# The first mixer of a two-block kernel: biases, products on ones, shift columns, and GpSimd's share of the splits

## The chip, the cores and the metric

The kernel runs on one core of one Trainium2 chip. The metric is the device time of one execution in microseconds. A core has five engines that run beside each other: TensorE (PE in the profile; PEld are its weight loads), VectorE (DVE), ScalarE (ACT), GpSimd (POOL) and SyncE (SP), which here only issues transfers (DMAs).

## The reference

Two transformer blocks over one sequence of 256 tokens of 1024 features. The change is in the first mixer, the first half of the first block:

```
mod = silu(c) @ w_ada + b_ada                  # 6 parts of 1024: sh1, sc1, g1, sh2, sc2, g2
h = rmsnorm(x, gain0) * (1 + sc1) + sh1
proj = h @ w_in                                # qa, ka, va (512 each), qb (512), kb, vb (128 each)
out_a = attention of 8 heads of 64 (causal, position bias)
out_b = windowed attention of 8 heads over 2 key heads, with sinks
x = x + g1 * rmsnorm(concat(out_a, out_b) @ w_out, gain1)
```

The second half is a feed-forward layer with its own scale and shift (sc2, sh2). The second block has two mixers and a mixture of 16 experts, whose weights (16 times 24 MB) are most of what is read.

## The kernel before

**Weights.** All weights pass through `Weights`: `unit` lists the transfers in the order of use, `pump` issues the next one on SyncE's queue as soon as its arena of SBUF chunks (1 MB each) has room, `done` gives chunks back when the last reader is through. Matrix products are made of three products of a rounded upper part and a remainder: `convert` casts a slice to its upper part on ScalarE (L228) and takes the remainder on VectorE or, for the slice numbers in `POOL_SPLITS`, on GpSimd (L232). Two slices are prepared ahead (`LOOK`). `mm3` issues upper x upper, upper x remainder and remainder x upper (L311 to L313).

**The modulation.** Six parts of `mod` are computed from `w_ada`. "sc" and "sh" come in four quarters of 1 MB, `quarter_step` makes their products on TensorE (L486) after two products that bring in the bias (L480); `summed` copies the sums out, `quarter_cols` turns them into columns of `modT` (L499, L501). "as" does the same in halves (`pe_step`, bias at L529, products at L534). "s2", "gA" and "ag" are accumulated on VectorE (L518), from a tile that GpSimd clears and fills with the bias (`begin`).

**The order of the first mixer.** x is normalised and transposed (xT); the scale's sums give A1 (L722). The keys (L746) run on xT scaled by A1, without the shift, in four groups k2 with three passes each; the quarters of the shift are put between the groups, and the product that makes the table of position biases (L760, L764, L776) after the third group. With the shift known, `scaled` writes the whole h = xT * A1 + sh as upper part and remainder (L664 to L666); the shift's product with the key weights is made apart (`shift_row`, L807, `shift_cols`, L817) and added to the keys as a bias. The queries `qa` (four tiles of 24 products) then run on h. After them `drive` interleaves two generators: `attention` (scores L903, softmax L914 to L934, transposes L944, values L958) and `proj_rest` (va, kvb, qb, the remaining parts of the modulation, the first half of w_out), as many steps of the second after each step of the first as `ATTENTION` says. The scaling of the softmax by the reciprocal sums is on GpSimd (L934). A tile of small vectors, VC, is transposed and copied on VectorE (L848) before the attention.

The tile framework puts each engine's instructions in an order of its own by estimated times and dependencies; `behind` names instructions after which the following ones are to be issued. Each engine works its queue in order.

Of the kernel before, what the change touches and what calls it, by code (L numbers as in the profile page):

```python
# [29 lines left out]
POOL_SPLITS = ((8, 10, 13, 15, 16, 17),  # L30
# [12 lines left out]
class Weights:  # L43
# [167 lines left out]
    def convert(self, upto):  # L211
        while self.conv < min(upto, len(self.slices)):
# [19 lines left out]
            eng.tensor_tensor(lo, src, hi.bitcast(F32), op=ALU.subtract)  # L232
# [28 lines left out]
def block_kernel(ctx: ExitStack, tc: tile.TileContext, x, c, w_in, w_out, sinks, rel_bias, w_ada, b_ada,  # L261
# [167 lines left out]
    bada = mod.tile([12, 512], F32, name="bada")  # L429
    nc.sync.dma_start(bada, b_ada[0].rearrange("(r f) -> r f", f=512))  # L430
# [4 lines left out]
    hsh = sp.tile([128, 8, S], F32R, name="hsh")  # L435
# [17 lines left out]

    p = tp_ps((128, 8))
# [13 lines left out]
    modT = const.tile([128, 48], F32, name="modT")  # L468
# [4 lines left out]
    def quarter_step(name, i, ps):  # L473


        t = W.raw(f"{name}{i}")
        if i == 0:
            r = 2 * PARTS.index(name)
            for j in range(2):
                mm(ps[32 * j:32 * j + 32, :], ident[0:12, r + j:r + j + 1].to_broadcast([12, 32]), bada,  # L480
                   start=True, stop=False, tile_position=(0, 32 * j))
        for kk in range(2):
            k = 2 * i + kk
            for j in range(2):
                b = 64 * kk + 32 * j
                mm(ps[b:b + 32, :], sc[:, k, :], t[:, kk, j * 512:(j + 1) * 512],  # L486
                   start=(k == 1), stop=(k >= 6))
        W.done(f"{name}{i}")
# [7 lines left out]
    def quarter_cols(name, m):  # L496
        ps = tp_ps((128, 4, 2))
        for b in range(4):
            mm(ps[:, b, :], m[:, b * 128:(b + 1) * 128], pairs, start=True, stop=True)  # L499
        i = 8 * PARTS.index(name)  # L500
        nc.vector.tensor_copy(modT[:, i:i + 8].rearrange("p (j b) -> p b j", j=2), ps)  # L501

    def begin(name, acc):

        if name in PE_PARTS:
            return
        ACC[name] = acc() if callable(acc) else acc
        acc = ACC[name]
        nc.gpsimd.memset(acc, 0.0)
        nc.gpsimd.dma_start(acc[0:1, :], flat(b_ada, D * PARTS.index(name), [[0, 1], [1, D]]))  # L510

    def step(name, i):
# [4 lines left out]
        for kk in range(w):  # L517
            nc.vector.scalar_tensor_tensor(ACC[name], t[:, kk, :], sc[:, w * i + kk, 0:1], ACC[name],  # L518
                                           op0=ALU.mult, op1=ALU.add)
        W.done(f"{name}{i}")  # L520

    def pe_step(name, i):
# [3 lines left out]
        if i == 0:  # L526
            r = 2 * PARTS.index(name)
            for j in range(2):
                mm(ps[32 * j:32 * j + 32, :], ident[0:12, r + j:r + j + 1].to_broadcast([12, 32]), bada,  # L529
                   start=True, stop=False, tile_position=(0, 32 * j))  # L530
        for kk in range(4):
            for j in range(2):
                b = 64 * (kk % 2) + 32 * j
                mm(ps[b:b + 32, :], sc[:, 4 * i + kk, :], t[:, kk, j * 512:(j + 1) * 512],  # L534
                   start=(kk == 1 if i == 0 else kk < 2), stop=(kk >= 2))
# [9 lines left out]
    def cols(name):  # L545
        if name in PE_PARTS:
            ps = tp_ps((128, 4, 2))
            for b in range(4):
                mm(ps[:, b, :], M[name][:, b * 128:(b + 1) * 128], pairs, start=True, stop=True)
            i = 8 * PARTS.index(name)  # L550
            nc.vector.tensor_copy(modT[:, i:i + 8].rearrange("p (j b) -> p b j", j=2), ps)
            return
# [4 lines left out]
        nc.vector.tensor_copy(modT[:, i:i + 8], ps)  # L557
# [136 lines left out]
    nc.vector.tensor_copy(nT, p0)  # L694
    for t in range(2):
# [24 lines left out]
    quarter_cols("sc", summed(msc))  # L720
    A1 = const.tile([128, 8], F32, name="A1")
# [8 lines left out]
    hs = (hsh, ap_.tile([128, 8, S], F32R, name="hsl", tag="ol"))  # L730
    kp = [b_ps((128, 256)) for _ in range(4)]

    def key_operands(k2):
        w = W.take(f"ka{k2 // 2}", 0)
        for k in (2 * k2, 2 * k2 + 1):
            nc.scalar.activation(hs[0][:, k, :], xT[:, k, :], AF.Copy, scale=A1[:, k:k + 1])
            nc.vector.scalar_tensor_tensor(hs[1][:, k, :], xT[:, k, :], A1[:, k:k + 1],
                                           hs[0][:, k, :].bitcast(F32), op0=ALU.mult, op1=ALU.subtract)
        return w

    def keys(k2, w, passes):
        for a, b in passes:
            for kk in range(2):
                k = 2 * k2 + kk
                for m in range(4):
                    mm(kp[m], w[a][:, kk, m * 128:(m + 1) * 128], hs[b][:, k, :],  # L746
                       start=(k == 0 and (a, b) == (0, 0)), stop=(k == 7 and (a, b) == (0, 1)))
# [9 lines left out]
    keys(2, ops[2], ALL)  # L757

    p = tp_ps((16, 384))
    mm(p, rb, pos, start=True, stop=True)  # L760
    bdist = sp.tile([16, 384], F32, name="bdist", tag="junk1")
    nc.vector.tensor_copy(bdist, p)
    fd = dram.tile([16, 384], F32, name="fd")
    nc.gpsimd.dma_start(fd, bdist)  # L764
# [4 lines left out]
    h = scaled(xT, A1, modT[:, 0:8])  # L769
# [50 lines left out]
    row = shift_row(["ka0", "ka1"], modT[:, 0:8], mod, "acc", 2)  # L820
    s0.close()
    wox = at.enter_context(tc.tile_pool(name="wox", bufs=2))
    as_ = ExitStack()
    aw = as_.enter_context(tc.tile_pool(name="attnw", bufs=2))
# [10 lines left out]
    qa = fm_block("qa", 4, h, put_q(0))  # L835
    next(qa)
# [7 lines left out]
    run(qa)  # L844
# [60 lines left out]
    def attn_soft(i):  # L905
# [144 lines left out]
    A2 = const.tile([128, 8], F32, name="A2")  # L1050
# [751 lines left out]
```

## Time and profile before

| | |
|---|---|
| median of 3 runs | 1499.63 us (1499.04 to 1503.82) |
| the profiled execution | 1499.25 us, its span 1497.5 us |
| TensorE, busy | 1120.5 us (75%) |
| VectorE, ScalarE, GpSimd, busy | 471.0, 303.9, 242.9 us |
| bytes moved | 513.59 MB, 343 GB/s over the span |
| mean clock granted to TensorE | 0.876 of full speed |

The span runs from the first to the last instruction; the rest of the execution's time lies around it. Busy shares are means over stages with different limits, so they are read stage by stage. The clock column of a stretch is the mean over two levels, 1.0 (2.4 GHz) and 0.5 (1.2 GHz).

### The profile page before, as it was taken

What the parts mean: (1) busy time and instruction counts of PE and PEld (TensorE: products, weight loads), DVE (VectorE), ACT (ScalarE), POOL (GpSimd) and SP (SyncE); (2) the same over time, 40 slices, a digit from 0 to 9 for tenths busy, and PEclk for the clock granted to TensorE, in tenths of its full rate; (3) what the DMA queues carried; (4) which work ended last, traced back from release to release, by engine and by line L of the source; (5) the groups of instructions that cost most, each with busy time, mean ns of one, the idle gap of its engine ahead of it and who ended that gap; (6) DMA issues with size and microseconds to landing.
All of it is one profiled execution on the core that took longest, in us unless ns stands there. A gap on an engine that the chain in (4) does not pass through costs nothing.

```text
span 1497.5 us, 16937 instructions
## 1 busy us (share of the span) xinstructions
PE 1120.5 (75%) x7125; PEld 625.3 (42%) x7125; DVE 471.0 (31%) x910; ACT 303.9 (20%) x535; POOL 242.9 (16%) x233
## 2 busy tenths in 40 slices
PE   7889999999989999964665665655656655665566
PEld 4675788897988896211111111111111111111122
DVE  3586667666788755100000000000000000000003
ACT  4436453454464652000000000000000000000000
POOL 1251253433335462000000000000000000000001
PEclk9999999999999999987788778888778879778887
DMA  9878346464335578999999999999999999999996
GB/s 359 306 296 297 112 172 239 173 222 170 121 137 202 196 281 328 415 431 433 430 429 430 432 426 433 430 431 426 432 427 433 432 428 431 431 428 432 433 418 233
DMA packets 69510, 513.59 MB, mean 343 GB/s; under 512 B 6178, under 2 KB 11443, under 8 KB 52026
## 3 DMA queue, kind: packets, MB, share of 16 engines
q1 hardware_dynamic: 67706, 508.27, 82.5%
q0 software_dynamic: 1440, 3.71, 0.8%
q8 instruction: 56, 0.92, 0.3%
q10 hardware_dynamic: 288, 0.52, 0.1%
q14 instruction: 20, 0.16, 0.0%
HBM read 511.42 MB, written 1.07 MB: 342 GB/s over the span
## 4 chain that ended last, share of the span: by engine, by line
DMA 49%; PE 37%; DVE 7%; POOL 2%; ACT 2%; issue 1%; POOLq 0%; SPq 0%; ACTq 0%; DVEq 0%
DMA wd<-in_w_down_e_dram 16%; DMA wd<-in_w_gate_e_dram 16%; DMA wd<-in_w_up_e_dram 16%; PE tp L1649 6%; PE f L1667 3%; PE f L311 3%; PE f L313 3%; PE f L312 3%; PE big L313 3%; PE big L312 3%; PE big L311 3%; DVE cy L1240 1%; DMA wa<-in_w_up_e_dram 1%; PE big L746 1%; PE tp L311 1%
## 5 line engine op out<-in xcount | busy, mean ns | idle before, releaser
L1649 PE MATMUL tp<-wa,work 128*32 128x512 f32 x1000 | 148.6, 744 | 105.3 <-DMA wa<-in_w_up_e_dram 82.2
L1657 DVE TENSOR_TENSOR work<-work,tp 128x512 f32<-128x512 f32 x16 | 11.0, 688 | 562.4 <-PE tp L1649 562.4
L1660 POOL TENSOR_SCALAR work<-iot,gi 128x256 f32<-128x256 f32 x16 | 14.8, 924 | 822.7 <-PE big L1701 805.2
L228 ACT CAST wboth<-wa 128x1024 fp32r<-128x1024 f32 x116 | 120.4, 1045 | 112.3 <-PE f L313 48.8
L1649 PE MATMUL tp<-wd,work 128*32 128x512 f32 x568 | 93.9, 797 | 62.6 <-DMA wd<-in_w_gate_e_dram 33.9
L232 DVE TENSOR_TENSOR wboth<-wa,wboth 128x1024 fp32r<-128x1024 f32 x92 | 116.3, 1271 | 56.3 <-ACT wboth L228 56.1
L311 PE MATMUL f<-hTh,wboth 128*128 128x256 f32 (+1 forms) x448 | 131.3, 293 | 2.6 <-ACT wboth L228 1.6
L313 PE MATMUL f<-hTh,wboth 128*128 128x256 f32 (+1 forms) x448 | 130.0, 290 | 2.2 <-DVE wboth L232 2.2
L312 PE MATMUL f<-hTl,wboth 128*128 128x256 f32 (+1 forms) x448 | 129.3, 289 | 0.0
L1649 PEld LDWEIGHTS tp<-wa,work 128*32 128x32 f32 x1000 | 35.3, 132 | 215.7 <-DMA wa<-in_w_up_e_dram 96.5
L1667 PE MATMUL f<-wa,work 128*32 128x512 f32 x472 | 74.3, 778 | 60.5 <-DMA wa<-in_w_down_e_dram 60.4
L1697 ACT ACTIVATE work<-f,gi 128x512 f32<-128x512 f32 x15 | 10.3, 687 | 537.0 <-PE f L1667 537.0
L1649 PE MATMUL tp<-we,work 128*32 128x512 f32 x384 | 62.8, 794 | 37.9 <-DMA we<-in_w_gate_e_dram 24.8
L311 PEld LDWEIGHTS f<-hTh,wboth 128*128 128x128 f32 x448 | 88.0, 196 | 4.1 <-ACT wboth L228 2.0
L1698 DVE TENSOR_SCALAR work<-f,gi 128x512 f32<-128x512 f32 x15 | 11.3, 750 | 248.0 <-PE f L1667 248.0
L313 PEld LDWEIGHTS f<-hTh,wboth 128*128 128x128 f32 x448 | 88.0, 196 | 2.7 <-DVE wboth L232 2.7
L312 PEld LDWEIGHTS f<-hTl,wboth 128*128 128x128 f32 x448 | 88.1, 197 | 0.1
L1649 PEld LDWEIGHTS tp<-wd,work 128*32 128x32 f32 x568 | 21.9, 141 | 132.2 <-issue 54.6
L232 POOL TENSOR_TENSOR wboth<-wa,wboth 128x1024 fp32r<-128x1024 f32 x24 | 59.3, 2475 | 65.6 <-ACT wboth L228 65.6
L1667 PE MATMUL f<-wd,work 128*32 128x512 f32 x256 | 49.6, 869 | 26.8 <-DMA wd<-in_w_down_e_dram 26.8
L1656 ACT ACTIVATE work<-tp 128x512 f32<-128x512 f32 x16 | 9.6, 597 | 292.4 <-PE tp L1649 292.4
L1667 PEld LDWEIGHTS f<-wa,work 128*32 128x32 f32 x472 | 19.6, 138 | 108.2 <-issue 103.8
(518 smaller groups left out, 1953.5 us busy)
## 6 DMA issues: line engine op xcount, KB each, us to landing
wa<-in_w_up_e_dram SPq DMA_DIRECT2D x15, 4096.0 KB, 33.8
wa<-in_w_down_e_dram SPq DMA_DIRECT2D x14, 4096.0 KB, 33.6
wa<-in_w_gate_e_dram SPq DMA_DIRECT2D x14, 4096.0 KB, 34.2
wa<-in_w_in_dram SPq DMA_DIRECT2D x14, 2048.0 KB, 7.5
wd<-in_w_down_e_dram SPq DMA_DIRECT2D x7, 4096.0 KB, 33.7
wd<-in_w_up_e_dram SPq DMA_DIRECT2D x7, 4096.0 KB, 33.6
wa<-in_w_dram SPq DMA_DIRECT2D x12, 2048.0 KB, 7.5
we<-in_w_gate_e_dram SPq DMA_DIRECT2D x8, 3072.0 KB, 36.0
```

The lines of the kernel that those rows point to most:

```text
L228: self.last = self.nc.scalar.copy(hi, src)
L232: eng.tensor_tensor(lo, src, hi.bitcast(F32), op=ALU.subtract)
L311: mm(o, a[0], b[0], start=start, stop=False)
L312: mm(o, a[0], b[1], start=False, stop=False)
L313: mm(o, a[1], b[0], start=False, stop=stop)
L746: mm(kp[m], w[a][:, kk, m * 128:(m + 1) * 128], hs[b][:, k, :], start=(k == 0 and (a, b) == (0, 0)), stop=(k == 7 and (a, b) == (0, 1)))
L1240: nc.vector.scalar_tensor_tensor(ys[k], zc[:, k, j:j + 256], vc(VC_CW, 8 * j + k), ys[k], op0=ALU.mult, op1=ALU.add)
L1649: LAST["pe"] = mm(ps[32 * j:32 * j + 32, :], xe[:, k, :], t[:, j * 512:(j + 1) * 512], start=(k == 0), stop=(k == 7))
L1657: nc.vector.tensor_tensor(hid, hid, pu, op=ALU.mult)
L1660: nc.gpsimd.tensor_scalar(oht, iot, gi[:, 1, e:e + 1], None, op0=ALU.is_equal)
L1667: mm(ps[32 * r:32 * r + 32, :], hT[:, 4 * j + r, :], ts[r][:, a:a + n], start=(j == 0), stop=(j == 3))
L1698: nc.vector.tensor_scalar(ye[1], pd[1], gi[:, 0, e:e + 1], None, op0=ALU.mult)
```

## The change

All edits are in the first mixer.

- *Biases.* `b_ada` is loaded as 48 rows of 128, transposed once on TensorE (`badaT`), and added where the columns are copied to `modT`. The bias products in `quarter_step` and `pe_step` and, for "s2", GpSimd's clearing and bias load go; the first step of "s2" writes the accumulator instead of adding to it.
- *Products on ones.* `warm_up` multiplies a tile of ones by a tile of ones into a bank that nobody reads: twelve products of 128 columns at the start, one of 256 columns behind the scale's sums, two behind the scale's columns.
- *The table product* is issued behind the keys of the third group.
- *Queries.* They run on the keys' operands `hs` (xT * A1), which get two more columns that hold the shift; a product of 258 columns gives the queries without the shift and, in column 256, the shift's part, which is scaled on VectorE and added as a bias on the way out (ScalarE). `scaled` still makes h for the later projections, behind the splits made so far. `shift_row` comes after the first tile of queries, and the pool of the keys' operands is closed after the queries.
- *GpSimd.* The six slices of the first mixer that it split go to VectorE; so does the softmax's scaling, as four instructions with a scalar per partition in place of two with a broadcast.
- `modT`, `A1` and `A2` move to another pool.

```diff
-POOL_SPLITS = ((8, 10, 13, 15, 16, 17),
+POOL_SPLITS = ((),
...
-            eng.tensor_tensor(lo, src, hi.bitcast(F32), op=ALU.subtract)
+            self.last_lo = eng.tensor_tensor(lo, src, hi.bitcast(F32), op=ALU.subtract)
...
-    bada = mod.tile([12, 512], F32, name="bada")
-    nc.sync.dma_start(bada, b_ada[0].rearrange("(r f) -> r f", f=512))
+    bada = sp.tile([48, 128], F32, name="bada")
+    nc.sync.dma_start(bada, b_ada[0].rearrange("(r f) -> r f", f=128))
...
+    def warm_up(n, w):
+
+        ps = b_ps()
+        for _ in range(n):
+            mm(ps[:, 0:w], ones, ones_w[:, 0:w], start=True, stop=True)
+
+    ones_w = sp.tile([128, 256], F32, name="ones_w")
+    nc.vector.memset(ones_w, 1.0)
+    warm_up(12, 128)
...
-        if i == 0:
-            r = 2 * PARTS.index(name)
-            for j in range(2):
-                mm(ps[32 * j:32 * j + 32, :], ident[0:12, r + j:r + j + 1].to_broadcast([12, 32]), bada,
-                   start=True, stop=False, tile_position=(0, 32 * j))
...
-        nc.vector.tensor_copy(modT[:, i:i + 8].rearrange("p (j b) -> p b j", j=2), ps)
+        nc.vector.tensor_tensor(modT[:, i:i + 8].rearrange("p (j b) -> p b j", j=2), ps,
+                                badaT[:, i:i + 8].rearrange("p (j b) -> p b j", j=2), op=ALU.add)
...
+    p0 = tp_ps((128, 48))
+    nc.tensor.transpose(p0, bada, ident[0:48, 0:48])
+    badaT = gpp.tile([128, 48], F32, name="badaT")
+    nc.vector.tensor_copy(badaT, p0)
...
-    quarter_cols("sc", summed(msc))
+    msc = summed(msc)
+    with behind("sums"):
+        warm_up(1, 256)
+    quarter_cols("sc", msc)
+    with behind("cols"):
+        warm_up(2, 256)
...
-    p = tp_ps((16, 384))
-    mm(p, rb, pos, start=True, stop=True)
...
+    with behind("keys"):
+
+        p = tp_ps((16, 384))
+        mm(p, rb, pos, start=True, stop=True)
...
-    h = scaled(xT, A1, modT[:, 0:8])
+    shift = modT[:, 0:8].rearrange("p (k o) -> p k o", o=1).to_broadcast([128, 8, 2])
+    nc.vector.tensor_copy(hs[0][:, :, S:HW], shift)
+    nc.vector.tensor_tensor(hs[1][:, :, S:HW], shift, hs[0][:, :, S:HW].bitcast(F32), op=ALU.subtract)
     keys(3, ops[3], ALL[1:])
...
-    qa = fm_block("qa", 4, h, put_q(0))
-    next(qa)
+
+    def queries(m):
+
+        ps = (f_ps, tp_ps)[m % 2]((128, HW))
+        fm_tile("qa", hs, ps)
+        bq = wk.tile([128, 1], F32, name="bq", tag="ms", bufs=4)
+        nc.vector.tensor_scalar(bq, ps[:, S:S + 1], 0.125, None, op0=ALU.mult)
+        nc.scalar.activation(qT[:, m, :].rearrange("p (t n) -> p t n", t=2),
+                             rev(ps[:, 0:S].rearrange("p (t n) -> p t n", t=2)), AF.Identity, scale=0.125, bias=bq)
+
+    queries(0)
+    row = shift_row(["ka0", "ka1"], modT[:, 0:8], mod, "acc", 2)
+    LAST["hi"], LAST["lo"] = W.last, W.last_lo
+    with behind("hi", "lo"):
+        h = scaled(xT, A1, modT[:, 0:8])
+    queries(1)
...
-    run(qa)
+    for m in range(2, 4):
+        queries(m)
+    s0.close()
...
-        for b, (o, n) in enumerate(((0, 128), (128, 256))):
-            nc.gpsimd.tensor_tensor(L[:, :, o:o + n], L[:, :, o:o + n],
-                                    rs[:, :, b:b + 1].to_broadcast([128, 2, n]), op=ALU.mult)
+        for u in range(2):
+            for b, (o, n) in enumerate(((0, 128), (128, 256))):
+                nc.vector.tensor_scalar(L[:, u, o:o + n], L[:, u, o:o + n], rs[:, u, b:b + 1], None, op0=ALU.mult)
```

## Rows read from the trace of the kernel before

**Rows 1.** The page: chain that ended last, shares by engine.
```profile
DMA 49%; PE 37%; DVE 7%; POOL 2%; ACT 2%; issue 1%; POOLq 0%; SPq 0%; ACTq 0%; DVEq 0%
```

**Rows 2.** Busy time by stage; last columns: clock, share of transfers, GB/s.
```profile
24.90:43.80 18.90, 18.83 (x128) 14.87 (x128) 7.27 (x12) 5.73 (x10) 1.57 (x2) 0.85 1.03 390
...
66.76:158.65 91.89, 84.81 (x517) 61.08 (x516) 69.40 (x140) 44.86 (x113) 31.54 (x23) 0.94 0.71 267
...
598.00:1497.00 899.00, 560.36 (x3534) 152.97 (x3534) 69.88 (x136) 22.48 (x35) 19.30 (x20) 0.81 0.99 421
```

**Rows 3.** The same view in two microseconds each, for the clock.
```profile
24.00:26.00 2.00, 1.07 (x5) 1.07 (x6) 1.97 (x5) 1.63 (x3) 0.52 (x1) 0.50 1.03 410
84.00:86.00 2.00, 2.00 (x7) 1.71 (x6) 1.66 (x4) 1.35 (x4) 0.08 (x1) 0.50 0.95 336
```

**Rows 4.** Timeline before the keys: start, length, engine, line, [idle before it, ended by].
```profile
21.86 1.04 ACT L228 CAST wboth<-wa 128x1024 fp32r<-128x1024 f32 x1 [4.20 <-DMA wa<-in_w_in_dram]
...
22.51 0.81 PE L760 MATMUL tp<-pos,rb 34*16 34x384 f32 x2
...
24.93 0.58 PE L746 MATMUL big<-hsh,wboth 128*128 128x256 f32 x1 [1.07 <-ACT hsh L736]
```

**Rows 5.** Timeline from the shift's sums to the first whole query product.
```profile
43.83 0.42 DVE L492 COPY m<-f 128x256 f32<-128x256 f32 x1 [10.27 <-PE f L486]
...
45.39 0.17 DVE L501 COPY modT<-tp 128x8 f32<-128x8 f32 x1 [0.81 <-PE tp L499]
...
45.62 1.92 PE L807 MATMUL f<-wa,modT 128*32 128x512 f32 x16 [0.26 <-DVE modT L501]
...
50.16 1.05 PE L817 MATMUL tp<-quad,row 128*128 128x1 f32 x8 [2.62 <-ACT row L811]
...
53.35 0.58 PE L313 MATMUL f<-hTh,wboth 128*128 128x256 f32 x1 [1.47 <-DVE wboth L232]
```

**Rows 6.** Timeline around TensorE's longest wait of the attention stage.
```profile
79.65 2.65 DVE L919 TENSOR_SCALAR nm<-mx 128x4 f32<-128x4 f32 x1
79.91 2.35 POOL L232 TENSOR_TENSOR wboth<-wa,wboth 128x1024 fp32r<-128x1024 f32 x1
82.21 1.27 DVE L518 SCALAR_TENSOR_TENSOR acc<-wa,sc,acc 128x1024 f32<-128x1024 f32 x1
...
83.71 0.90 PE L944 MATMUL tp<-ident,L 128*128 128x128 f32 x3 [3.92 <-DVE VC L848]
```

**Rows 7.** Timeline of VectorE: scaling 512 columns in SBUF.
```profile
9.06 0.49 DVE L700 TENSOR_SCALAR xn<-X,rs 128x512 f32<-128x512 f32 x1 [0.24 <-POOL rs L589]
```

**Rows 8.** Transfers of the first 70 us: count, size, median us to landing.
```profile
wb<-in_w_ada_dram SPq DMA_DIRECT2D x2, 1024.0 KB, 16.1
```

**Rows 9.** Timeline of issues: third and fourth shift quarter, bias tables.
```profile
17.00 2.86 SPq L149 DMA_DIRECT2D wb<-in_w_ada_dram  x2
...
29.16 1.57 POOL L776 DMA_DIRECT2D tb<-fd  x2 [4.45 <-DMA fd<-bdist]
```

**Rows 10.** Groups by shape, 60 to 165 us: count | busy, mean ns | idle.
```profile
L518 DVE SCALAR_TENSOR_TENSOR acc<-wa,sc,acc 128x1024 f32<-128x1024 f32 x12 | 17.8, 1483 | 0.2
...
L232 POOL TENSOR_TENSOR wboth<-wa,wboth 128x1024 fp32r<-128x1024 f32 x6 | 15.5, 2588 | 16.2 <-ACT wboth L228 16.1
L232 DVE TENSOR_TENSOR wboth<-wa,wboth 128x1024 fp32r<-128x1024 f32 x12 | 14.8, 1254 | 8.6 <-ACT wboth L228 8.6
...
L934 POOL TENSOR_TENSOR L<-L,rsm 128x512 f32<-128x512 f32 x8 | 10.3, 1283 | 0.0
...
L919 DVE TENSOR_SCALAR nm<-mx 128x4 f32<-128x4 f32 x8 | 4.5, 561 | 0.2
...
L529 PE MATMUL f<-bada,ident 12*32 12x512 f32 x4 | 2.4, 672 | 0.0
```

**Rows 11.** Timeline of TensorE among the queries, first and last of 56.
```profile
60.13 0.28 PE L313 MATMUL f<-hTh,wboth 128*128 128x256 f32 x1
...
66.56 0.28 PE L313 MATMUL f<-hTh,wboth 128*128 128x256 f32 x1
```

More of the change, by code (lines that the diff above doesn't have):

```diff
@@ L485, in quarter_step @@
                 b = 64 * kk + 32 * j
-                mm(ps[b:b + 32, :], sc[:, k, :], t[:, kk, j * 512:(j + 1) * 512],
-                   start=(k == 1), stop=(k >= 6))
+                LAST["sums"] = mm(ps[b:b + 32, :], sc[:, k, :], t[:, kk, j * 512:(j + 1) * 512],
+                                  start=(k < 2), stop=(k >= 6))
         W.done(f"{name}{i}")
@@ L498, in quarter_cols @@
         for b in range(4):
-            mm(ps[:, b, :], m[:, b * 128:(b + 1) * 128], pairs, start=True, stop=True)
+            LAST["cols"] = mm(ps[:, b, :], m[:, b * 128:(b + 1) * 128], pairs, start=True, stop=True)
         i = 8 * PARTS.index(name)
-        nc.vector.tensor_copy(modT[:, i:i + 8].rearrange("p (j b) -> p b j", j=2), ps)
+        nc.vector.tensor_tensor(modT[:, i:i + 8].rearrange("p (j b) -> p b j", j=2), ps,
+                                badaT[:, i:i + 8].rearrange("p (j b) -> p b j", j=2), op=ALU.add)
     def begin(name, acc):
@@ L507, in begin @@
         ACC[name] = acc() if callable(acc) else acc
+        if name == "s2":
+            return
         acc = ACC[name]
@@ L517, in step @@
         for kk in range(w):
+            if name == "s2" and i == kk == 0:
+                nc.vector.tensor_scalar(ACC[name], t[:, 0, :], sc[:, 0, 0:1], None, op0=ALU.mult)
+                continue
             nc.vector.scalar_tensor_tensor(ACC[name], t[:, kk, :], sc[:, w * i + kk, 0:1], ACC[name],
@@ L525, in pe_step @@
         ps = f_ps()
[L526 to L530, printed above, removed]
         for kk in range(4):
@@ L534, in pe_step @@
                 mm(ps[b:b + 32, :], sc[:, 4 * i + kk, :], t[:, kk, j * 512:(j + 1) * 512],
-                   start=(kk == 1 if i == 0 else kk < 2), stop=(kk >= 2))
+                   start=(kk < 2), stop=(kk >= 2))
         W.done(f"{name}{i}")
@@ L546, in cols @@
         if name in PE_PARTS:
[L547 to L552, printed above, removed]
+            return quarter_cols(name, M[name])
         ps = tp_ps((128, 8))
@@ L735, in key_operands @@
         for k in (2 * k2, 2 * k2 + 1):
-            nc.scalar.activation(hs[0][:, k, :], xT[:, k, :], AF.Copy, scale=A1[:, k:k + 1])
-            nc.vector.scalar_tensor_tensor(hs[1][:, k, :], xT[:, k, :], A1[:, k:k + 1],
-                                           hs[0][:, k, :].bitcast(F32), op0=ALU.mult, op1=ALU.subtract)
+            nc.scalar.activation(hs[0][:, k, 0:S], xT[:, k, :], AF.Copy, scale=A1[:, k:k + 1])
+            nc.vector.scalar_tensor_tensor(hs[1][:, k, 0:S], xT[:, k, :], A1[:, k:k + 1],
+                                           hs[0][:, k, 0:S].bitcast(F32), op0=ALU.mult, op1=ALU.subtract)
         return w
@@ L745, in keys @@
                 for m in range(4):
-                    mm(kp[m], w[a][:, kk, m * 128:(m + 1) * 128], hs[b][:, k, :],
-                       start=(k == 0 and (a, b) == (0, 0)), stop=(k == 7 and (a, b) == (0, 1)))
+                    LAST["keys"] = mm(kp[m], w[a][:, kk, m * 128:(m + 1) * 128], hs[b][:, k, 0:S],
+                                      start=(k == 0 and (a, b) == (0, 0)), stop=(k == 7 and (a, b) == (0, 1)))
     ALL = ((0, 0), (1, 0), (0, 1))
@@ L843, in block_kernel @@
             nc.vector.tensor_scalar(kT[:, m, :], kp[m], bk[:, m:m + 1], None, op0=ALU.add)
-    run(qa)
+    for m in range(2, 4):
+        queries(m)
+    s0.close()
+    wox = at.enter_context(tc.tile_pool(name="wox", bufs=2))
+    as_ = ExitStack()
+    aw = as_.enter_context(tc.tile_pool(name="attnw", bufs=2))
     p = tp_ps((128, 104))
```

25 lines of the change are left out of this document (10 added, 15 removed).

## The prediction

> **What bounds the kernel now.** I read the chain of waits first: it puts about half of the span on expert weights in flight and the rest mostly on TensorE [rows 1]. The stage windows say where which holds: after 598 us the transfers are busy 0.99 of the time at 421 GB/s and nothing but bytes sets the pace; until 158.65 they have idle time left in the attention stage (0.71) [rows 2]. An expert weight can only be issued when a buffer of an earlier weight is released, and those are released by the projections. So the last 900 us are a fixed block that starts when the work before it is done, and a microsecond taken out of the first mixer is a microsecond off the end. The change lies wholly in the first 160 us, so I read three stretches there: the keys (24.9 to 43.8), the wait and the queries (to 66.76), the attention stage (to 158.65).
>
> In the keys stretch the reader should see two things: the clock column (0.85 over the stretch, 0.50 in its first microseconds [rows 2, 3]) and what precedes the first key product, the cast of the key weights at 21.86, which waited for its transfer [rows 4]. In the second stretch: the shift columns are ready at 45.56, and the first query product that has both halves of its weights runs at 53.35, behind the splitting of the scaled operands and behind the weights' remainder [rows 5]. In the attention stage VectorE is busy 69.4 of 91.9 us [rows 2], and TensorE's longest wait, 3.92 us, ends with a VectorE copy that stood behind a four-column instruction of 2.65 us [rows 6].
>
> **The change part by part.** The sum is made against the profiled execution: 1499.25 us (span 1497.5); the median of the runs is 0.4 above it, which is nothing here. A difference under 0.3% (4.5 us) can't be told from no change.
>
> *Bias products before the keys.* The scale loses its two bias products on TensorE. What can be collected of them is capped: the key weights land at 21.86 whatever TensorE does, their cast takes 1.04, so the first key product can start at 22.9 and not at 24.93: 2.0 us [rows 4]. The new bias transpose (one, where two like it already stand at the start) and the addition in place of a copy cost nothing visible: VectorE and TensorE wait for transfers there. If that cover were gone they would cost some 0.2 us each, the price of the 128x8 copy [rows 5]. The twelve opening products lie before the first operand has landed; nothing waits for them.
>
> *Products on ones.* The keys stretch had a mean clock of 0.85, so (1-0.85)/0.5 = 0.30 of 18.9 us, 5.7 us, ran at 1.2 GHz instead of 2.4; that costs half of it, 2.8 us [rows 2, 3]. TensorE had been mostly waiting just before the rate fell. Three filled products in that gap can save between 0 and 2.8; I take 2.8, because keys also start two microseconds earlier, so that the gap itself is shorter. Against it, the table product with its 0.81 us moves into this stretch [rows 4]. The shift's sums thus end at 43.8-2.0-2.8+0.8 = 39.8.
>
> *Queries with the shift as two columns.* Today the shift columns come 1.76 us after the sums (45.56 against 43.8) [rows 5]: 41.6 in the new order. Two small VectorE instructions on 128x16 follow; between the 0.17 us of 128x8 [rows 5] and the 0.49 us of 128x512 [rows 7] I take 0.3 each: 42.2. But the query weights must be there too. The third shift quarter lands 16.1 us after an issue at 17.0, at 33.1 [rows 8, 9]; the fourth (1 MB) and the query weights (2 MB) follow at 390 GB/s [rows 2], 2.7 us per MB: 41.2. Cast 1.04 [rows 4] and remainder 1.25 [rows 10] make 43.5. The bias tables (1 MB, issued at 29.16 today [rows 9]) are then no longer in front, since their product moves behind three key groups; if they were, 46.2. So the first whole query product comes at 43.5 instead of 53.35, and the transfer, not the shift, decides it. The split of the other operands still takes its time, but beside the queries.
>
> The queries themselves: 96 products. Between 60.13 and 66.56 there are 55 starts, 0.117 us each [rows 11], so 11.2 us; two columns more are under a hundredth of each. The shift row (1.92) and its columns (1.05) [rows 5], which today fill the wait, now stand among them: 14.2, and 0.5 for the copies out: 58.2. Today the attention starts at 66.76 [rows 2]. **First term: -8.6 us.**
>
> *GpSimd gives up splits and scaling.* Here the wait of 3.92 us goes [rows 6]: the instruction in front of the copy was stretched while a GpSimd split ran beside it, and the copy now comes right behind the queries. The stage's clock of 0.94 means (1-0.94)/0.5 x 91.9 = 11 us at 1.2 GHz, up to 5.5 us lost; one of the low stretches starts in that wait and covers the products after it [rows 3]. I take back 2.5. The bias products of the fifth modulation part go: 2.4 us [rows 10]. Together -8.8. VectorE pays: six splits at 1.25 [rows 10] and, for eight head pairs, two scalings of 128 and two of 256 columns. By 0.17 for 8 columns and 0.49 for 512 [rows 5, 7] these are 0.25 and 0.33, 1.16 a pair; in all 7.5+9.3 = 16.8 us. It gets back what GpSimd stretched: twelve accumulations at 1.48 instead of 1.27, 2.5 us, and eight four-column instructions at 0.56 instead of 0.17, 3.1 us [rows 5, 6, 10]. Its load goes to 69.4+16.8-5.6 = 80.6 us in a stage of 91.9-8.8 = 83.1: 97%. It works in order, so some TensorE waits come back. No row prices that; the ends are 0 and the whole 8.8. I take 2.3, nearer to zero, because the sixteen accumulations are wanted only at the end of the stage and pieces of the weights are split two ahead. **Second term: -6.5 us.**
>
> The Trainium skill (page "SBUF — State Buffer", section "Who interferes with whom") says that a GpSimd instruction and a VectorE instruction with two SBUF inputs, or in a two-port mode, exclude each other for the whole instruction. The trace agrees in the 2.65 us row [rows 6]. By that rule all of the 25.8 us of GpSimd work in two rows [rows 10] could have kept VectorE out, its load would fall and the 2.3 would go: 1482. By the rows only 5.6 us were lost, and I stay with them.
>
> Sum: 1499.25-8.6-6.5 = 1484.1; **1484 us**.
>
> **The rivals.** (a) *VectorE becomes the bound.* At 97% load the second term is eaten: -8.6 alone, 1490.6. For it: the load; against it: the first term doesn't depend on it. (b) *Transfers and clock hold the first term.* Tables in front of the query weights (+2.7) and the rate falling all the same (+2.8): -3.1-6.5, 1489.7. For it: the transfer engines are busy all through the keys stretch (1.03) [rows 2]. The Trainium skill (page "TensorE: Matmul & The Clock Gate", section "Why this matters for your kernels") asks for TensorE to be kept busy without gaps for the full rate; by it three short products may not do, which alone would make 1487. (c) *Slower: the scaling waits in VectorE's queue.* Today GpSimd begins it when the reciprocal is done; on VectorE it can stand behind two accumulations and a split, 2x1.48+1.25 = 4.2 us, and eight rounds of it are 33.7 us, against 17.4 gained (8.6+8.8): 1515. It decides from 2.7 us a round ((17.4+4.5)/8). Against it: TensorE has other products between rounds. (d) *The start moves but not the end*: 1499. For it: half of the chain is transfers [rows 1]; against it: the transfers have idle time in the attention stage, so they wait for buffers [rows 2].
>
> **How the numbers follow.** My forecast (1479 to 1488) 0.52, (a) 0.20, (b) 0.15, (d) 0.07, (c) 0.06. The low end takes the second term without its charge and with all 5.5 of the clock, -8.6-8.8-3.0 = -20.4, and one more from the first, where 0.5 for copies and 0.5 of the remainder might lie beside other work: 1477.9, set to 1477. The high end takes the late query weights (-5.9) and no second term: 1493. That leaves out (c), (d) and little else. Faster: 0.52+0.20+0.15 = 0.87; within 0.3%: 0.07; slower: 0.06.
>
> **What would show it.** First key product near 22.9 and a clock above 0.9 between keys and queries; first query product with its remainder at 43 to 44, right behind the query weights' landing; attention from about 58; no TensorE wait of 3 us in the attention stage, VectorE above 90% busy there, its four-column instructions near 0.17; attention stage near 85 us; and the expert stage as long as today, begun 15 us earlier. Wrong would be: a TensorE wait for the scaling in every round, or an expert stage that is longer by what the front gained.

## The result, and the profile after

| | before | after |
|---|---|---|
| median of 4 runs each, same chip | 1501.72 us (1499.04 to 1504.03) | 1477.87 us (1477.06 to 1485.89) |
| the profiled execution | 1499.25 us, span 1497.5 | 1478.44 us, span 1476.6 |
| first key product | 24.93 us | 24.55 us |
| first whole query product | 53.35 | 45.12 |
| first score of the attention | 66.77 | 59.62 |
| first instruction of the residual | 162.16 | 141.81 |
| first expert transposition | 598.13 | 578.21 |

The ratio is 0.985, with a 95% interval of 0.981 to 0.989: faster by 1.1 to 1.9%. The forecast was 1484, in a range of 1477 to 1493, so that the median lies 0.9 us above its low end. The start came out 7.1 us earlier where 8.6 were forecast. The attention stage (here from its first score to the first instruction of the residual, 95.4 us before) lost 13.2 us where 6.5 were forecast. What comes behind it kept its length: 436.0 and 436.4 us to the experts, then 899.4 and 898.4.

The chain of waits of after, its shares by engine, answers to [rows 1]:

```profile
DMA 52%; PE 36%; DVE 6%; POOL 2%; ACT 1%; issue 1%; SPq 1%; POOLq 0%; ACTq 0%; DVEq 0%
```

The busy time of after by stage answers to [rows 2]; the rows are the keys, the queries, the attention stage and the experts, the columns those of [rows 2]:

```profile
24.55:43.71 19.16, 18.54 (x139) 13.54 (x139) 8.75 (x16) 7.45 (x12) 2.08 (x3) 1.00 1.04 397
43.71:59.63 15.92, 15.92 (x121) 13.23 (x121) 14.08 (x30) 10.24 (x18) 1.48 (x2) 1.00 1.05 379
59.63:141.81 82.18, 81.67 (x544) 62.28 (x544) 71.95 (x180) 45.57 (x115) 1.54 (x2) 1.00 0.87 328
...
579.10:1476.00 896.90, 555.52 (x3530) 152.83 (x3522) 69.81 (x135) 22.48 (x35) 19.31 (x20) 0.81 0.99 422
```

In all three stages of the first mixer TensorE is now busy nearly all the time (81.67 of 82.18 us in the attention stage), and the clock stands at 1.00. VectorE is busy 71.95 of 82.18 us, 88%: it took over the scaling and the splits and has hardly more to do than the 69.40 of [rows 2]. The expert stage again sets its pace by bytes.

Before the keys, answering to [rows 4]; the timeline of after:

```profile
19.48 1.07 PE L490 MATMUL big<-wa,sc 128*32 128x512 f32 x8 [1.83 <-DMA wa<-in_w_ada_dram]
...
22.39 0.17 DVE L731 SCALAR_TENSOR_TENSOR A<-modT,nT 128x8 f32<-128x8 f32 x1
22.66 0.91 ACT L745 ACTIVATE hsh<-xT,A 128x256 fp32r<-128x256 f32 x2 [6.47 <-DVE A L731]
23.47 1.99 ACT L228 CAST wboth<-wa 128x1024 fp32r<-128x1024 f32 x2
...
24.55 0.61 PE L755 MATMUL big<-hsh,wboth 128*128 128x256 f32 x3 [1.43 <-ACT wboth L228]
```

The scale's last sums wait for their own transfer until 19.48, and on ScalarE two scaled operands went ahead of the weights' cast, which begins at 23.47 and not at 21.86. That is why the first key product gained 0.4 us and not 2.0. In the row of [rows 4] it was the scaled operand (`ACT hsh`), not the cast, that the first key product waited for; here it is the cast.

From the shift's sums to the first whole query product, answering to [rows 5]:

```profile
41.59 2.94 ACT L228 CAST wboth<-wa 128x1024 fp32r<-128x1024 f32 x3 [11.70 <-PE f L490]
...
43.60 0.18 DVE L781 TENSOR_TENSOR hsl<-modT,hsh 128x16 fp32r<-128x16 f32 x1
...
43.71 0.36 PE L311 MATMUL f<-hsh,wboth 128*128 128x258 f32 x1 [0.56 <-ACT wboth L228]
43.77 2.36 DVE L232 TENSOR_TENSOR wboth<-wa,wboth 128x1024 fp32r<-128x1024 f32 x2
...
45.12 0.39 PE L313 MATMUL f<-hsh,wboth 128*128 128x258 f32 x1
```

The query weights are cast from 41.59 (41.2 forecast). The row puts the end of that wait down to the shift's last sums, which end at 41.54, so it doesn't show that the transfer decides here, as forecast; in the experiment with the table product in front it does. The weights' remainder stands on VectorE behind the two shift instructions, which end at 43.78, and so the first product with both halves runs at 45.12 (43.5 forecast).

VectorE's groups in the attention stage of after, by shape, answer to [rows 10]; the fourth row has its like in [rows 6]:

```profile
L232 DVE TENSOR_TENSOR wboth<-wa,wboth 128x1024 fp32r<-128x1024 f32 x15 | 18.1, 1221 | 0.3 <-ACT wboth L228 0.2
L528 DVE SCALAR_TENSOR_TENSOR acc<-wa,sc,acc 128x1024 f32<-128x1024 f32 x12 | 15.4, 1280 | 0.0
...
L961 DVE TENSOR_SCALAR L<-L,rsm 128x256 f32<-128x256 f32 x16 | 5.6, 348 | 0.0
...
L945 DVE TENSOR_SCALAR nm<-mx 128x4 f32<-128x4 f32 x8 | 1.3, 158 | 0.0
```

The accumulation fell from 1483 to 1280 ns, the four-column instruction from 561 to 158. Four more accumulations of before, which [rows 10] do not show, were longer still; three of them now take 1279 ns, and the fourth is a write:

```profile
L518 DVE SCALAR_TENSOR_TENSOR acc<-wb,sc,acc 128x1024 f32<-128x1024 f32 x4 | 7.0, 1744 | 0.0
```

### The profile page after: what moved, and what is told of

Same layout as the page of the kernel before. It is cut to its first block, busy times and chain, and to the rows that moved or that the text cites. A ratio compares the mean times of both kernels' runs of the same rounds, so it can differ in the third digit from the quotient of the medians.

```text
span 1476.6 us, 16973 instructions
## 1 busy us (share of the span) xinstructions
PE 1109.5 (75%) x7144; PEld 625.0 (42%) x7144; DVE 474.5 (32%) x956; ACT 304.4 (21%) x537; POOL 209.2 (14%) x209
## 4 chain that ended last, share of the span: by engine, by line
DMA 52%; PE 36%; DVE 6%; POOL 2%; ACT 1%; issue 1%; SPq 1%; POOLq 0%; ACTq 0%; DVEq 0%
DMA we<-in_w_gate_e_dram 17%; DMA we<-in_w_up_e_dram 16%; DMA we<-in_w_down_e_dram 16%; PE tp L1675 5%; PE big L311 3%; PE big L313 3%; PE big L312 3%; PE f L311 3%; PE f L313 3%; PE f L312 3%; PE f L1693 3%; DMA wa<-in_w_ada_dram 2%; SPq L147 1%; PE tp L311 1%; PE tp L312 1%
## 5 line engine op out<-in xcount | busy, mean ns | idle before, releaser
L232 DVE TENSOR_TENSOR wboth<-wa,wboth 128x1024 fp32r<-128x1024 f32 x98 | 123.1, 1263 | 46.7 <-ACT wboth L228 46.5
L1693 PE MATMUL f<-wa,work 128*32 128x512 f32 x472 | 77.5, 808 | 62.6 <-DMA wa<-in_w_down_e_dram 62.5
L311 PE MATMUL f<-hTh,wboth 128*128 128x256 f32 (+1 forms) x416 | 119.8, 288 | 1.6 <-ACT wboth L228 1.6
L313 PE MATMUL f<-hTh,wboth 128*128 128x256 f32 (+1 forms) x416 | 118.9, 286 | 1.5 <-POOL wboth L232 0.8
L312 PE MATMUL f<-hTl,wboth 128*128 128x256 f32 (+1 forms) x416 | 118.1, 284 | 0.0
L1675 PE MATMUL tp<-we,work 128*32 128x512 f32 x384 | 59.5, 757 | 35.9 <-DMA we<-in_w_gate_e_dram 23.1
L311 PEld LDWEIGHTS f<-hTh,wboth 128*128 128x128 f32 x416 | 79.5, 191 | 2.9 <-ACT wboth L228 2.0
L313 PEld LDWEIGHTS f<-hTh,wboth 128*128 128x128 f32 x416 | 79.6, 191 | 2.1 <-POOL wboth L232 1.0
L312 PEld LDWEIGHTS f<-hTl,wboth 128*128 128x128 f32 x416 | 79.7, 192 | 0.4 <-issue 0.3
L1693 PEld LDWEIGHTS f<-wa,work 128*32 128x32 f32 x472 | 20.7, 143 | 112.7 <-issue 110.2
L1727 PE MATMUL big<-work 128*128 128x512 f32 x120 | 55.4, 603 | 4.3 <-ACT work L1723 3.8
```

Source lines behind the costliest of these rows:

```text
L232: self.last_lo = eng.tensor_tensor(lo, src, hi.bitcast(F32), op=ALU.subtract)
L311: mm(o, a[0], b[0], start=start, stop=False)
L312: mm(o, a[0], b[1], start=False, stop=False)
L313: mm(o, a[1], b[0], start=False, stop=stop)
L1675: LAST["pe"] = mm(ps[32 * j:32 * j + 32, :], xe[:, k, :], t[:, j * 512:(j + 1) * 512], start=(k == 0), stop=(k == 7))
L1693: mm(ps[32 * r:32 * r + 32, :], hT[:, 4 * j + r, :], ts[r][:, a:a + n], start=(j == 0), stop=(j == 3))
```

## The experiments

Theory G, formed on these rows: GpSimd's work in the attention stage cost far more than the forecast gave it, by holding VectorE up, and its going is what the extra 6.7 us are. The rival, theory Q: the new queries (a shorter, denser start) did it, and the stage got faster because it begins with a full clock and nothing left over. All kernels are edits of after, but for the fourth, an edit of before.

**GpSimd's two parts, undone together, singly, and done alone.**

```diff
-POOL_SPLITS = ((),
+POOL_SPLITS = ((8, 10, 13, 15, 16, 17),          # splits back
...
-        for u in range(2):
-            for b, (o, n) in enumerate(((0, 128), (128, 256))):
-                nc.vector.tensor_scalar(...)
+        for b, (o, n) in enumerate(((0, 128), (128, 256))):
+            nc.gpsimd.tensor_tensor(...)           # scaling back
```

Both back:

> The changed kernel with GpSimd's share given back (the six splits and the scaling). Theory G (GpSimd held VectorE up, and that is most of what the attention stage gained beyond the forecast): the attention stage grows from 82.2 us by 7 to 10, four-column instructions are over 0.4 us again, 1485 to 1488. Theory Q (the stage gained by the new order in front of it and by the missing bias products): the stage grows by 2 at most, 1478 to 1480.

The splits alone back:

> The changed kernel with only the six splits back on GpSimd. Theory G: they are 15.5 of the 32.7 us that GpSimd worked in the stage and the ones that ran beside the 2.65 us row: +4 to +6, 1482 to 1484. Theory Q: within 1 us of the changed kernel.

The scaling alone back:

> The changed kernel with only the softmax's scaling back on GpSimd. Theory G: +2 to +4 (five waits of 2.0 us in all on it before, and some stretch), 1480 to 1482. Theory Q: within 1 us. If VectorE's load at 88% were what limits the stage, it would be faster, 1475 to 1477.

The two edits alone, made in the kernel before:

> The kernel before with only GpSimd's two edits. Theory G: the wait of 3.9 us and the low clock after it go, -8 to -10 from before: 1490 to 1492. Theory Q: the edits need the new order, -3 at most: 1497 to 1500.

Measured: 1493.77, 1481.41, 1487.91 and 1488.63 us (ratios to before 0.995 [0.993, 0.997], 0.987 [0.986, 0.989], 0.992 [0.991, 0.994], 0.992 [0.990, 0.994]). The attention stage, each row from one window and the clock's records of one execution, in us:

```
kernel                 stage  TensorE busy  idle  at half rate  VectorE busy  GpSimd busy
before                  95.4      88.3       7.1      10.2          70.2         31.5
both back               94.0      87.5       6.5      10.2          65.3         32.3
scaling back            89.4      84.2       5.2       3.4          68.1         18.5
splits back             85.3      82.8       2.5       3.4          72.8         15.9
GpSimd edits alone      84.4      84.0       0.4       3.4          72.5          1.6
after                   82.2      81.7       0.5       0            72.0          1.5
```

Theory Q falls: with the new queries kept and GpSimd's work put back, the stage is 94.0 us, and with the old queries and only GpSimd's work gone it is 84.4. The scaling counts more than the splits (7.2 against 3.1 us alone), and together they make 11.8. So GpSimd's work is the cause, but theory G had its parts wrong: it expected 7 to 10 us for both, 4 to 6 for the splits, 2 to 4 for the scaling and 8 to 10 for the edits alone (12.3 in the medians), and its sign of a held VectorE, the four-column instruction over 0.4 us again, did not come. In both back it is short, and VectorE is less busy (65.3 us) than in any other row of the table:

```profile
L945 DVE TENSOR_SCALAR nm<-mx 128x4 f32<-128x4 f32 x8 | 1.5, 187 | 0.1
```

The two largest waits of TensorE in that stage of both back (the line that waits, what ends the wait: us in total, times, longest):

```profile
PE f L313 <- POOL wboth L232: 2.8, 1, 2.8
PE tp L970 <- POOL L L960: 2.4, 5, 0.7
```

the largest of scaling back:

```profile
PE tp L970 <- POOL L L960: 4.4, 6, 1.6
```

and the largest of splits back:

```profile
PE tp L984 <- DVE PT L973: 1.9, 2, 1.7
```

In after the same view has one line, 0.2 us, and no GpSimd in it. So with the scaling on GpSimd TensorE waits for GpSimd's own results, and with both parts back once for a split, too; with the splits alone no wait names GpSimd, and the two that there are name VectorE, whose accumulations are back at 1564 ns. Beside the waits, both back ran 10.2 us at half rate; TensorE was busy in 9.4 of them, which costs half of that, 4.7. Waits and clock together (6.0 more of idle time and 4.7) are 10.7 of the 11.8 us.

**The same work on GpSimd, with nobody waiting for it.** Lateness is one way in which GpSimd can cost; what it does to VectorE beside it is another.

```diff
+        for b, (o, n) in enumerate(((0, 128), (128, 256))):
+            nc.gpsimd.tensor_tensor(Z[:, :, 0:n], Z[:, :, 0:n],
+                                    rs[:, :, b:b + 1].to_broadcast([128, 2, n]), op=ALU.mult)
```

> The changed kernel with, beside VectorE's scaling, the two multiplications of a step put on GpSimd as well, on a scratch tile that nobody reads (sizes 2 x 128 and 2 x 256, as in the kernel before; the output is the reference's). Theory L (the scaling on GpSimd cost by its lateness: TensorE waited for it, and its clock fell after the waits): the attention stage stays at 82 to 84 us, against 82.2 without the idle work and 89.4 with the scaling moved back, no wait of TensorE over 0.35 us names GpSimd, and the time is 1478 to 1481. Theory P (GpSimd's work cost by what it did to VectorE beside it): the four-column instruction goes from 158 to over 200 ns in the mean, VectorE's split and scaling lengthen, and the stage goes to 87 to 92 us, 1484 to 1489 in all.

Measured: 1484.92 us (0.990 [0.988, 0.992]); the profiled execution was the longest of the five, 1492.19. In it the stage takes 87.9 us with VectorE busy 80.4, TensorE idle 4.4 and no stretch at the low clock. Theory P has the size right and the place wrong: the four-column instruction keeps its 159 ns, and what lengthens is VectorE's own scaling, which here begins at the same moment. Two rows of VectorE's groups by shape in this stage:

```profile
L963 DVE TENSOR_SCALAR L<-L,rsm 128x128 f32<-128x128 f32 x16 | 12.5, 781 | 0.1
...
L963 DVE TENSOR_SCALAR L<-L,rsm 128x256 f32<-128x256 f32 x16 | 6.9, 432 | 0.0
```

and the first step in its timeline, the second row being four scalings of VectorE:

```profile
71.89 1.85 POOL L965 TENSOR_TENSOR Z<-Z,rsm 128x256 f32<-128x256 f32 x2 [6.69 <-DVE rsm L960]
...
71.95 2.14 DVE L963 TENSOR_SCALAR L<-L,rsm 128x128 f32<-128x128 f32 x4
```

In after these four take 1.00 us (from 67.54). TensorE's largest wait in the stage, in total, is for this scaling:

```profile
PE tp L975 <- DVE L L963: 2.4, 6, 0.7
```

So GpSimd instructions whose results nobody reads, sixteen with 15.7 us in all, cost 5.7 us of stage because VectorE stands beside them. The rule cited in the prediction (the Trainium skill, page "SBUF — State Buffer", section "Who interferes with whom": such pairs exclude each other) agrees with these rows. What part of the 7.2 us of scaling back is lateness and what part this, the runs don't separate: there the GpSimd instruction whose result TensorE awaits is itself one of the pair.

**The bias products of the fifth part**, put back on a tile of zeros:

```diff
+        if i == 0:
+            for j in range(2):
+                mm(ps[32 * j:32 * j + 32, :], ident[0:12, j:j + 1].to_broadcast([12, 32]), zb,
+                   start=True, stop=False, tile_position=(0, 32 * j))
```

> The changed kernel with the two bias products of the attention scale put back at the head of its sums, on a tile of zeros (12 rows by 512; the output is the reference's, as the transposed biases are still added). If these products account for the rest of the stage that the two GpSimd edits leave (84.4 against 82.2 us), the stage goes to 84 to 85 us and the time to 1480 to 1481; the products themselves are expected at 4 x 0.6 us as before the change. If the rest is the clock (a 3.4 us stretch at half rate is worth 1.7), the stage stays within 0.7 us of 82.2, or rises only where a stretch at the low clock appears in it.

Measured: 1481.84 us (0.987 [0.986, 0.989]), stage 84.9, where 84 to 85 was expected if the products account for the rest. But it is about a third products and two thirds clock. The timeline of TensorE in this kernel:

```profile
103.94 1.04 PE L538 MATMUL f<-zb,ident 12*32 12x512 f32 x2
104.91 1.92 PE L543 MATMUL f<-wb,sc 128*32 128x512 f32 x16
...
113.32 1.55 PE L311 MATMUL big<-wboth,oh 128*128 128x512 f32 x4
```

and its clock, in two microseconds each:

```profile
112.00:114.00 2.00, 2.00 (x12) 1.57 (x13) 1.42 (x4) 0.00 (x0) 0.00 (x0) 0.99 1.05 390
114.00:116.00 2.00, 2.00 (x9) 1.60 (x8) 2.00 (x3) 0.00 (x0) 0.00 (x0) 0.50 1.04 384
```

One pair of bias products takes 103.94 to 104.91, 0.97 us; the other pair runs where after has two products of the sums, and adds nothing. The low clock behind it lasts 3.4 us and costs 1.7. After has 1.00 there. Products and clock, 0.97 and 1.7, make the 2.7 us. No wait stands before this low stretch: TensorE is busy in 2.00 of the 2.00 us ahead of it. That the products bring it is not shown. It lies at the same place in the kernel with the GpSimd edits alone, which has these products too, but also in scaling back (114.5 to 117.9), which has not. None of the other six kernels with after's attention code (the five of the start and the last one, all below) has a low stretch in this stage.

**The start: each of its edits undone.** Without all the products on ones (`warm_up` and its three calls removed):

> The changed kernel without any product on ones. If they hold the clock between the scale and the keys (the forecast's 2.8 us): the rate falls near 24 us, the shift's sums come 2.5 to 3 us later and, as the query weights land at 41.5 anyway, the attention starts 2 to 3 us later, at 62: 1480 to 1481. If the order and not the ones keeps the rate: no low stretch there and within 1 us of the changed kernel.

Without the three in the gap; the twelve at the opening stay:

```diff
-    with behind("sums"):
-        warm_up(1, 256)
     quarter_cols("sc", msc)
-    with behind("cols"):
-        warm_up(2, 256)
```

> The changed kernel without the three products on ones in the gap between the scale's sums and the first key product; the twelve at the opening stay. If the three do it, as forecast: the low clock starts near 21 us again and covers the first keys, the first whole query product comes at 47 to 48 us as without all fifteen (47.78), and the time is 1480 to 1484. If the twelve at the opening do it (they move the low stretch of the start forward, so that it is over before the gap): the low stretch lies at 9 to 16 us as in the changed kernel, the first whole query product stays at 45 to 45.5, and the time is 1477 to 1480.

Measured: 1483.90 us (0.988 [0.983, 0.992]; 1480 to 1481 was expected) and 1482.14 us (0.987 [0.985, 0.989]). The first whole query product comes at 47.78 and 47.22 against 45.12, the scores at 62.73 and 62.66 against 59.62, the residual at 144.9 and 144.8 against 141.8: 3 us, and the same with and without the twelve. Half of it is there at the shift's columns (45.65 against 44.14 without the three), half comes from a second low stretch behind them (46.0 to 49.4). The clock without the three, in two microseconds each:

```profile
22.00:24.00 2.00, 0.01 (x1) 0.00 (x0) 1.22 (x4) 1.49 (x3) 0.00 (x0) 0.52 1.05 392
24.00:26.00 2.00, 1.59 (x7) 1.59 (x8) 1.61 (x2) 2.00 (x4) 0.00 (x0) 0.50 1.04 414
```

and in after:

```profile
22.00:24.00 2.00, 1.12 (x6) 0.67 (x5) 1.14 (x4) 1.34 (x3) 0.00 (x0) 1.00 1.06 400
24.00:26.00 2.00, 1.40 (x9) 1.19 (x10) 1.55 (x3) 2.00 (x4) 0.00 (x0) 1.00 1.02 403
```

So the twelve do nothing that shows, and the low stretch over the keys goes with the three. They are no guarantee. Of the ten kernels traced with the three the clock fell over the first keys in four: both back (24.6 to 28.0 us), idle scaling (19.8 to 30.0) and, below, the queries back (20.6 to 30.8) and the cast put first (20.7 to 27.5). Of the four traced without them (before, the GpSimd edits alone, and these two) it fell in all.

The queries on the whole scaled operand, as before the change:

```diff
-    shift = modT[:, 0:8].rearrange(...)
-    nc.vector.tensor_copy(hs[0][:, :, S:HW], shift)
-    nc.vector.tensor_tensor(hs[1][:, :, S:HW], shift, ..., op=ALU.subtract)
+    h = scaled(xT, A1, modT[:, 0:8])
...
-    queries(0)
...
+    qa = fm_block("qa", 4, h, put_q(0))
+    next(qa)
```

> The changed kernel with the queries on the whole h again (scaled before them, shift row and columns in front, the pool closed early). Theory P (the split of the whole h stood in the way): first whole query product at 50 to 52 instead of 45.1, TensorE idles for 3 us or more before it, attention from 64 to 66, 1483 to 1486. Rival (the transfer of the query weights and the clock decide): at most +2, 1480.

Measured: 1486.42 us (0.989 [0.985, 0.994]). The shift's columns are first used at 46.43 (44.14 in after, the keys at a low clock here) and the first whole query product runs at 54.72 (50 to 52 expected):

```profile
46.43 1.93 PE L817 MATMUL f<-wa,modT 128*32 128x512 f32 x16 [0.26 <-DVE modT L505]
...
54.72 0.58 PE L313 MATMUL f<-hTh,wboth 128*128 128x256 f32 x1 [1.49 <-DVE wboth L232]
```

That is 8.3 us behind the columns, against 1.0 in after. The scores start at 67.58, 8.0 us late; 2.3 of them were there at the columns, and the other 5.7 are what the two columns save, a low stretch from 51.3 to 58.1 in the wait among them. The stage is 83.1 us: the queries are the start's gain, not the stage's.

The table product back in front of the keys (its `with behind("keys")` removed), and the weights' cast ahead of the two operands on ScalarE:

```diff
+        LAST["hi"] = W.last
         for k in (2 * k2, 2 * k2 + 1):
-            nc.scalar.activation(hs[0][:, k, 0:S], xT[:, k, :], AF.Copy, scale=A1[:, k:k + 1])
+            with behind("hi"):
+                nc.scalar.activation(hs[0][:, k, 0:S], xT[:, k, :], AF.Copy, scale=A1[:, k:k + 1])
```

> The changed kernel with the product for the bias tables not tied to the keys of the third group. The forecast's view: the tables (1 MB) are in front of the query weights, whose cast starts 2.5 us later than 41.6, and the first whole query product at 46 to 47.5: 1479 to 1480. Rival: the queue takes them side by side and only the sums count: within 1 us, or faster by the 0.8 that TensorE saves among the keys.

> The changed kernel with each cast of key weights issued on ScalarE ahead of the scaled operands of its group (the first cast stands behind two of them now and starts at 23.47, though its weights land at about 21). Theory: the first key product at 23.5 instead of 24.55, all after it 1 us earlier, 1476.5 to 1477.5. Rival: the scale's columns at 22.4 decide and it moves by under 0.3 us.

Measured: 1482.08 us (0.986 [0.982, 0.991]) and 1478.20 us (0.984 [0.979, 0.988]). With the table in front, the timeline shows the query weights late, a little later than the 46 to 47.5 expected for the whole product:

```profile
44.47 2.94 ACT L228 CAST wboth<-wa 128x1024 fp32r<-128x1024 f32 x3 [14.76 <-DMA wa<-in_w_in_dram]
...
48.14 0.58 PE L313 MATMUL f<-hsh,wboth 128*128 128x258 f32 x1
```

The cast comes 2.9 us later than in after and ends a wait for a transfer, the whole product 3.0 us later: the tables' megabyte in front of the weights, priced at 2.7 in the prediction. In that wait the clock fell as well (43.3 to 50.1). With the cast first, it begins at 21.85 and the first key product at 23.99, 0.56 earlier than in after (23.5 expected), but only 0.2 to 0.4 earlier than in five other variants whose start is after's (24.17 to 24.37). The cast ends at 22.89, where the prediction put the first key product; the scaled operand comes later:

```profile
23.14 0.91 ACT L747 ACTIVATE hsh<-xT,A 128x256 fp32r<-128x256 f32 x2 [0.25 <-DVE A L731]
```

The low clock took the gain back, and the time is after's.

**All other splits off GpSimd too** (20 of the later weights):

```diff
-POOL_SPLITS = ((),
-               (2, 6, 9, 10, 11, 13, 15, 16, 19, 26, 27, 28, 30, 32, 37, 39, 40, 41, 50, 54))
+POOL_SPLITS = ((), ())
```

> The changed kernel with the 20 splits of the later weights taken from GpSimd too, so that VectorE splits all. Theory G carried on (GpSimd's late splits hold TensorE up wherever they stand): the stretch from the first residual to the expert's first transposition, 437 us, or the tail, 897.5 us, gets shorter by 2 to 10 us, 1468 to 1476 in all. Rival: in the later stretches VectorE is the later of the two engines, or the weights arrive no earlier, so that the splits on GpSimd are cover and not a hold: 20 splits at 1.28 us are 25.6 us more on VectorE, of which some 5 to 25 us come through, 1483 to 1503.

Measured: 1466.85 us (0.979 [0.977, 0.981] of before), a little beyond the end of theory G and 11.0 below after's median (9.6 by the two ratios to before). It is the fastest kernel of the study. The first expert transposition comes at 566.35 instead of 578.21 us; the tail keeps its 898.7. Groups of VectorE from 142 to 580 us, first after:

```profile
L232 DVE TENSOR_TENSOR wboth<-wa,wboth 128x1024 fp32r<-128x1024 f32 x73 | 93.0, 1278 | 44.9 <-ACT wboth L228 44.8
L1266 DVE SCALAR_TENSOR_TENSOR cy<-zc,VC,cy 128x256 f32<-128x256 f32 x32 | 24.4, 811 | 0.6 <-ACT cy L1263 0.4
...
L1471 DVE SCALAR_TENSOR_TENSOR dl<-dl,ds 128x256 f32<-128x256 f32 x8 | 10.2, 1277 | 3.2 <-POOL dl L1470 3.2
```

then this kernel (its lines stand one higher):

```profile
L231 DVE TENSOR_TENSOR wboth<-wa,wboth 128x1024 fp32r<-128x1024 f32 x91 | 113.4, 1250 | 41.6 <-ACT wboth L227 41.6
L1265 DVE SCALAR_TENSOR_TENSOR cy<-zc,VC,cy 128x256 f32<-128x256 f32 x32 | 14.2, 476 | 0.2
...
L1470 DVE SCALAR_TENSOR_TENSOR dl<-dl,ds 128x256 f32<-128x256 f32 x8 | 3.9, 483 | 3.3 <-POOL dl L1469 3.3
```

Eighteen more splits of this group are 20.4 us of work, and the two other rows alone give 16.5 back. The busy time from the residual to about the first expert work, in after:

```profile
141.81:579.10 437.29, 420.64 (x2731) 372.21 (x2733) 302.87 (x573) 208.57 (x342) 179.94 (x169) 0.98 0.53 197
```

and in this kernel:

```profile
141.63:566.60 424.97, 415.74 (x2726) 367.65 (x2728) 303.81 (x593) 209.21 (x342) 130.00 (x149) 1.00 0.55 202
```

VectorE's busy time rises by 0.9 us for 20 splits (the durations added up by 2.6), GpSimd's falls by 50, TensorE's idle time by 7.4 us (16.65 to 9.23), and its busy time by 4.9 at the better clock. TensorE is busy 98% of the stretch; little is left there for this kind of edit.

## Why the prediction was right, and where its sizes were off

Direction and place were right: start and attention stage both got shorter, and what follows passed the gain on (20.4 us at the residual, 20.9 in the span). Two terms were mis-sized, in opposite senses, and that they partly cancel is luck. The median, 1477.87, lies outside the 1479 to 1488 that had the chance of 0.52; the range holds it because its low end left VectorE's charge out and took all of the clock's loss back, which is much of what happened. Of the signs, those of the start's times (first key product near 22.9, first whole query product at 43 to 44, attention from about 58) and VectorE above 90% failed. The clock, the four-column instruction, no wait of 3 us and the unchanged expert stage came.

- *First term, -8.6; measured -7.1.* The step that failed is the first key product at 22.9: the cast was taken to start at 21.86, as [rows 4] show, but in the new order two operands stand ahead of it on ScalarE, and it was 24.55; and the scaled operand, which the row of [rows 4] names, was given no time. The bias products of scale and shift were not put back by any run. The steps behind it nearly held their distances: the sums ended at 41.54 (39.8), the first whole query product was at 45.12 (43.5), and from there to the scores it took 14.5 us (14.7). The tables' transfer (2.7) came out as worked out, 3.0, and the query weights' cast began at 41.59 (41.2). The three products (2.8) were worth 3.0 at the scores, but only 1.5 of that lies in the keys, which is what the 2.8 priced; the rest is a second low stretch behind them that the prediction did not have.
- *Second term, -6.5; measured -13.2.* Three pieces, from the table above. TensorE's idle time fell by 6.6 us (7.1 to 0.5), not only by the one wait of 3.92, so that the charge of 2.3 for VectorE wasn't paid. All of the half-rate time in the stage went: 10.2 us, in which TensorE was busy for 8.4, so 4.2 us, of which 2.5 were taken. The bias products gave 1.0 and not 2.4, since one of the two pairs only changed places with other products. Together 11.8 of 13.2; the other 1.4 us of TensorE's busy time are not placed.
- *The step that failed there* is VectorE's load of 97%: 80.6 us were worked out and 71.95 measured. It was given back 5.6 us of stretched instructions for 16.8 us of new work. The accumulations went to 1280 ns, as forecast, and the four-column instruction to 158; but GpSimd had lengthened others too: by group and shape the stretching in the stage was 9.1 us (accumulations 4.0, four-column instructions 3.2, splits 1.3, sums 0.6). The prediction counted twelve of the sixteen accumulations and left out the four that were stretched most, 1744 ns. The rest is in the counting. The durations of VectorE's instructions in the stage, added up, rose from 78.3 to 84.5 us: 16.2 of new work (five splits and the scaling), 9.1 less of stretching, 0.8 less because the first accumulation is now a write (0.74 us, begun just ahead of the stage). But time in which two instructions overlap in the records is busy once, and so busy time rose from 70.25 to 71.95 only. With the load at 88% no TensorE wait over 0.35 us came back.
- *Rivals.* (a) VectorE as the bound: no, 88%. (b) the transfers and the clock: neither happened in after; the transfers cost their price when the table product was moved back, and the clock fell over the keys in eight of the other thirteen kernels traced, four of them with the three products. (c) the scaling in VectorE's queue: no wait of TensorE for it in after. (d) the end doesn't move: it moved by all that the start gained. The alternative by the Trainium skill (page "SBUF — State Buffer", section "Who interferes with whom"), 1482, went the right way from 1484 and not far enough.

The four runs of after spread over 8.8 us, and a trace shows one execution, so of the differences of 2 or 3 us between variants only those are read that the traces place.

## What to carry to other kernels

When work moves from GpSimd to VectorE, don't add its price to VectorE's load: look up what VectorE's neighbouring instructions cost where GpSimd is quiet, and count the difference for all of them. Look also at who waits for GpSimd's own results: with the scaling on GpSimd such waits were 4.4 us where the stage lost 7.2. Then count TensorE's short waits together, and the low-clock time in the stage, and not only the longest wait. And if one stage gains this way, try the same edit in the next; here that gave another 10 to 11 us.

## What the hardware showed that I had not expected

- VectorE took 20 more splits, 25 us by their mean, for 0.9 us more busy time. A three-operand VectorE instruction of 128x256 took 811 ns in the mean beside GpSimd's splits and 476 without.
- A GpSimd instruction on a tile that nobody reads lengthened VectorE's 128x128 scaling from 283 to 781 ns and the stage by 5.7 us.
- Three short products on numbers that nobody reads, in a gap of some 2 us, went with a clock of 1.00 over the keys in after and were worth 3 us in the trace. With the same products the clock fell over the keys in four of ten kernels. Why it holds in one execution and not in another stays open.
- The clock fell to 0.50 in the attention stage with no wait before it: TensorE was busy in 2.00 of the 2.00 us ahead, and in 13.97 of 14.00 us around the same place of scaling back (104 to 118).
